# Turning the second pair of hidden column blocks two steps earlier in three feed-forward stages of a hybrid decoder trunk

## The chip, the cores and the metric

The kernel runs on one core of a Trainium2 chip. TensorE (PE in the profile) multiplies matrices, VectorE (DVE) and ScalarE (ACT) do elementwise work, GpSimd (POOL) does a little of it and issues some DMAs, SyncE (SP) issues the weight loads. Each engine works through its own instructions in order and waits for the others through semaphores. The metric is the device time of one execution in microseconds (us). Beside plain timed executions there is one execution recorded by the hardware profiler; its trace is what the views below are taken from.

## The reference

Two layers over 256 tokens of width 1024, everything in float32. Each layer is: a SwiGLU feed-forward (FFN), a token mixer (sparse attention in layer 0, a Mamba-2 scan in layer 1), and a second FFN; after each of the three, a LayerNorm of the scaled residual plus the result. The FFN, which this case is about, is

```python
def swiglu_ffn(x, w_in, w_out):
    gate, up = jnp.split(x @ w_in, 2, axis=-1)
    return (jax.nn.silu(gate) * up) @ w_out
```

with 2816 hidden columns, that is 22 column blocks of 128. There are four FFNs; the mixers lie between the first and second and between the third and fourth.

## The kernel before

**Weights.** A product in float32 is made as three faster passes (`mm3`, L540 to L543): every operand is split into a high part H and a low part L, and H·H, H·L and L·H are added up in one PSUM bank. A weight unit is a 128x1024 tile: SP loads it (`raw`), ACT rounds it to its high part `wh` (L338), DVE subtracts to get the low part `wl` (L363). At most ten units are made ahead of their use. `W.pump`, called once in every step, first emits the low parts of units whose high parts are out, then makes new high parts, then emits sums of raw weight tiles where a block of products needs them (DVE, L305, or an accumulating DMA that POOL issues, L278).

**An FFN.** The 22 column blocks go in this order. First `WIDE = 2` pairs of blocks are made with the tokens on the output rows (`wide`); w = 0 is blocks 0 and 1, w = 1 is blocks 2 and 3. In the FFNs other than the first, four groups of four column blocks follow, each made with seven products in place of eight (a Strassen-type scheme; `seven`). The products of a group are called A11, Q1, S2, Q4, S3, A12 and A22; in the first group of an FFN they run in this order, 12 matmuls each. The last two column blocks are made singly (`one`). In between and behind, `out_pieces` multiplies finished hidden blocks with rows of `w_out` into four accumulator banks `acc00`, `acc01`, `acc10`, `acc11` (two token halves by two column halves), 12 matmuls for each piece, three for each bank. The first group has only two such pieces in it: piece 0 between A12 and A22, piece 1 behind A22.

**Turning.** Hidden values of the wide pairs have tokens on the rows, while `out_pieces` needs columns on the rows. So `tr(w)` (L772) transposes the four 128x128 blocks on PE into one PSUM bank, ACT copies the bank to the high part `hH` (L780), and DVE subtracts to get the low part `hL` (L781), reading the bank as well. For the two wide pairs that bank has the name `pht` and takes the place of an accumulator: w = 0 uses `acc10`, w = 1 uses `acc11`. The accumulators are first written in piece 0, whose last three matmuls go to `acc11`; the tile allocator lets them start only when the bank's earlier reader, the `hL` subtraction, is done.

**What sets the order.** The order is written out by hand through a queue of steps. `later(f, d)` puts work into the d-th step from now, `step()` runs the work of the step that is due and then pumps weights, and there is one step behind each product and each out piece. When the second half of a wide pair is multiplied (`mul`, L789), `tr(w)` is put into the queue; `tr` emits transposes and the ACT copy at once and its DVE subtraction goes to the next step. With a delay of five, counted from the end of the wide products: step one is behind Q1 (it holds `tr(0)`, counted from its own, earlier product), two behind S2, three behind Q4, four behind S3, five behind A12. Step six is behind piece 0. At these places stand also `c12` (L931, emitted in step three), `c22` (L936, step four) and `c11` (L941, step five), subtractions and additions on DVE that put the products together, and the SiLU calls (L787) on ACT.

Of the kernel before, what the change touches and what calls it, by code (L numbers as in the profile page):

```python
# [65 lines left out]
WIDE = 2  # L66
# [353 lines left out]
def trunk_kernel(ctx: ExitStack, tc: tile.TileContext, widths, forms, x, ln_g, ln_b, wts, kvg, convp,  # L420
# [12 lines left out]
    def nm(s):  # L433
        cnt[0] += 1
        return f"{s}_{cnt[0]}"
# [7 lines left out]
    def f1(s):  # L443
        return wk.tile([128, 256], F32, name=nm(s), tag="f1", bufs=6)
# [23 lines left out]
    def ptr():  # L468
        return psum.tile([128, 512], F32, name=nm("ptr"), tag="ptr", bufs=2)
# [276 lines left out]
    def ffn(xT, u0, ln_i, first=False, last=False, ff=False, seven_at=SEVEN):  # L746
# [9 lines left out]
        def later(f, d=1):  # L756

            while len(queue) < d:
                queue.append([])
            queue[d - 1].append(f)  # L760
# [11 lines left out]
        def tr(w):  # L772

            pt = psum.tile([128, 512], F32, name=nm("pht"), tag=f"acc1{w}", bufs=1) if w < WIDE else ptr()
            for t in range(2):
                h = ready.pop((t, w))
                for i in range(2):
                    nc.tensor.transpose(pt[:, i * 256 + t * 128:i * 256 + (t + 1) * 128], h[:, i * 128:(i + 1) * 128],
                                        ident)
            nc.scalar.copy(hH[w], pt)  # L780
            return lambda: nc.vector.tensor_sub(hL[w], pt, hH[w].bitcast(F32))  # L781

        def glu(t, w, c, sil=None):


            g, h = (c[:, :256], c[:, 256:]) if sil is None else (sil, f1("h"))
            nc.scalar.activation(g, c[:, :256], AF.Silu)  # L787

            def mul():  # L789
                nc.vector.tensor_mul(h, c[:, 256:], g)  # L790
                W.owe(800)
                ready[t, w] = h
                if (1 - t, w) in ready:
                    later(lambda: later(tr(w)), 5 if w < WIDE and not first else 2)

            later(mul)

# [971 lines left out]
```

## Time and profile before

| what | value |
|---|---|
| timed executions | 1034.69, 1034.94 and 1036.64 us, median 1034.94 us |
| profiled execution | 1036.55 us |
| its span, first to last instruction | 1034.4 us |
| what lies around the span | 2.15 us |
| PE, DVE, ACT busy (share of the span) | 98%, 88%, 63% |
| mean granted TensorE clock | 0.992 |
| second, third and fourth FFN, from the trace | about 289 to 456, 470 to 636 and 845 to 1028 us |

In a row of the timeline the columns are start, duration, engine, line, operation, output<-inputs, shape, count of merged instructions, and in brackets the idle time of the engine just before with what ended it. PE rows give matmuls, whose modelled durations overlap; the distance from start to start is what counts. In a table of windows each engine has its busy time and, in brackets, its number of instructions; PEclk is the granted TensorE clock, 1.00 being full speed. In the list of waits the columns are total, number of times and longest wait, in us.

### The profile page before, as it was taken

What the parts mean: (1) busy time and instruction counts of PE and PEld (TensorE: products, weight loads), DVE (VectorE), ACT (ScalarE), POOL (GpSimd) and SP (SyncE); (2) the same over time, 40 slices, a digit from 0 to 9 for tenths busy, and PEclk for the clock granted to TensorE, in tenths of its full rate; (3) what the DMA queues carried; (4) which work ended last, traced back from release to release, by engine and by line L of the source; (5) the groups of instructions that cost most, each with busy time, mean ns of one, the idle gap of its engine ahead of it and who ended that gap; (6) DMA issues with size and microseconds to landing.
All of it is one profiled execution on the core that took longest, in us unless ns stands there. A gap on an engine that the chain in (4) does not pass through costs nothing.

```text
span 1034.4 us, 14640 instructions
## 1 busy us (share of the span) xinstructions
PE 1013.6 (98%) x5319; PEld 855.2 (83%) x5319; DVE 911.2 (88%) x1282; ACT 650.5 (63%) x945; POOL 105.4 (10%) x164
## 2 busy tenths in 40 slices
PE   8999999999999999999999999999999999999996
PEld 7888888898787888888788888999889888788885
DVE  6789997788799899979989997789999879989986
ACT  6666675476657666754766675486766546677660
POOL 2011000100001110000111000140111111010001
PEclk9999999999999999999999999999999999999998
DMA  9769998252638889791988988355555645889751
GB/s 334 281 148 286 270 336 294 85 181 75 210 103 243 215 276 276 262 332 66 249 210 282 272 270 286 126 171 193 174 176 178 221 171 121 266 285 261 239 192 42
DMA packets 62505, 223.85 MB, mean 216 GB/s; under 512 B 7040, under 2 KB 7104, under 8 KB 62432
## 3 DMA queue, kind: packets, MB, share of 16 engines
q1 hardware_dynamic: 51264, 183.43, 49.3%
q0 software_dynamic: 10880, 38.96, 18.7%
q8 instruction: 42, 0.69, 0.3%
q10 hardware_dynamic: 288, 0.52, 0.1%
q14 instruction: 31, 0.25, 0.1%
HBM read 193.48 MB, written 1.08 MB: 188 GB/s over the span
## 4 chain that ended last, share of the span: by engine, by line
PE 81%; DVE 10%; ACT 4%; issue 3%; DMA 1%; POOL 0%; SPq 0%; POOLq 0%; DVEq 0%; ACTq 0%
PE pmm L543 10%; PE pmm L541 10%; PE pmm L542 10%; PE acc L541 9%; PE acc L543 9%; PE acc L542 9%; DVE wl L363 4%; ACT wh L338 2%; PE pmm L690 2%; PE ptr L690 2%; PE pxs L541 1%; PE pxs L543 1%; PE pxs L542 1%; PE ptr L542 1%; PE ptr L543 1%
## 5 line engine op out<-in xcount | busy, mean ns | idle before, releaser
L363 DVE TENSOR_TENSOR wl<-raw,wh 128x1024 fp32r<-128x1024 f32 (+2 forms) x422 | 495.2, 1213 | 13.6 <-ACT wh L338 13.3
L338 ACT CAST wh<-raw 128x1024 fp32r<-128x1024 f32 (+2 forms) x424 | 423.1, 1044 | 108.7 <-DVE raw L305 68.9
L541 PE MATMUL acc<-wh,hH 128*128 128x512 f32 (+1 forms) x352 | 139.0, 395 | 7.2 <-DVE hL L781 7.2
L543 PE MATMUL acc<-wh,hL 128*128 128x512 f32 (+1 forms) x352 | 137.3, 390 | 0.0
L542 PE MATMUL acc<-wl,hH 128*128 128x512 f32 (+1 forms) x352 | 137.1, 389 | 0.0
L541 PE MATMUL pmm<-wh,xT 128*128 128x512 f32 (+2 forms) x312 | 123.8, 397 | 0.0
L542 PE MATMUL pmm<-wl,xT 128*128 128x512 f32 (+2 forms) x312 | 120.8, 387 | 0.7 <-DVE wl L363 0.7
L543 PE MATMUL pmm<-wh,xT 128*128 128x512 f32 (+2 forms) x312 | 121.1, 388 | 0.2 <-DVE xT L538 0.2
L278 POOL DMA_DIRECT2D raw<-raw x54 | 47.0, 870 | 408.3 <-DVE raw L305 216.7
L541 PE MATMUL pmm<-wh,xf 128*128 128x512 f32 x216 | 84.4, 391 | 0.1
L543 PE MATMUL pmm<-wh,xf 128*128 128x512 f32 x216 | 84.1, 389 | 0.0
L542 PE MATMUL pmm<-wl,xf 128*128 128x512 f32 x216 | 84.0, 389 | 0.0
L541 PEld LDWEIGHTS acc<-wh,hH 128*128 128x128 f32 x352 | 66.3, 188 | 21.1 <-DVE hL L781 8.5
L305 DVE TENSOR_TENSOR raw<-raw,raw 128x1024 f32<-128x1024 f32 x66 | 79.3, 1220 | 0.4
L543 PEld LDWEIGHTS acc<-wh,hL 128*128 128x128 f32 x352 | 66.4, 189 | 14.0
L542 PEld LDWEIGHTS acc<-wl,hH 128*128 128x128 f32 x352 | 66.5, 189 | 12.5
L543 PEld LDWEIGHTS pmm<-wh,xT 128*128 128x128 f32 x312 | 59.3, 190 | 13.5 <-DVE xT L538 1.6
L542 PEld LDWEIGHTS pmm<-wl,xT 128*128 128x128 f32 x312 | 59.8, 192 | 12.3 <-DVE wl L363 1.4
L541 PEld LDWEIGHTS pmm<-wh,xT 128*128 128x128 f32 x312 | 59.8, 192 | 10.9
L541 PEld LDWEIGHTS pmm<-wh,xf 128*128 128x128 f32 x216 | 40.5, 188 | 8.6 <-ACT c L948 0.3
L543 PEld LDWEIGHTS pmm<-wh,xf 128*128 128x128 f32 x216 | 40.5, 188 | 8.5
L542 PEld LDWEIGHTS pmm<-wl,xf 128*128 128x128 f32 x216 | 40.5, 188 | 8.4
(322 smaller groups left out, 1848.4 us busy)
## 6 DMA issues: line engine op xcount, KB each, us to landing
raw<-in_wts_dram SPq DMA_DIRECT2D x339, 512.0 KB, 5.3
raw<-raw POOLq DMA_DIRECT2D x54, 512.0 KB, 6.1
M<-scr POOLq DMA_DIRECT2D x8, 512.0 KB, 5.2
lng<-in_ln_g_dram POOLq DMA_DIRECT2D x6, 512.0 KB, 5.1
lnb<-in_ln_b_dram POOLq DMA_DIRECT2D x6, 512.0 KB, 5.3
raw<-in_wts_dram SPq DMA_DIRECT2D x4, 408.0 KB, 5.3
out_dram<-x SPq DMA_DIRECT2D x4, 256.0 KB, 2.1
raw<-in_wts_dram SPq DMA_DIRECT2D x2, 492.0 KB, 5.2
```

Source lines behind the costliest of these rows:

```text
L278: self.nc.gpsimd.dma_start(self.raw[r], self.raw[other], accum_op=ALU.add)
L305: self.nc.vector.tensor_add(self.raw[r], self.raw[r], self.raw[other])
L338: nc.scalar.copy(h[:, c:c + n], raw[:, c:c + n])
L363: self.nc.vector.tensor_sub(lo[:, s], raw[:, s], h[:, s].bitcast(F32))
L541: nc.tensor.matmul(ps, lh, rh, start=first, stop=False, skip_group_check=on)
L542: nc.tensor.matmul(ps, lh, rl, start=False, stop=False, skip_group_check=on)
L543: nc.tensor.matmul(ps, ll, rh, start=False, stop=last, skip_group_check=on)
L690: nc.tensor.matmul(ps, H[:, k * 128:(k + 1) * 128], xT.HL[:, k, :], start=k == 0, stop=False)
```

## The change

One expression, in `mul` inside `glu`. The delay of `tr(w)` becomes 5 for w = 0 (as before) and 3 for w = 1. In the first FFN (`first`) and for all other pairs it stays 2.

```diff
                 W.owe(800)
                 ready[t, w] = h
                 if (1 - t, w) in ready:
-                    later(lambda: later(tr(w)), 5 if w < WIDE and not first else 2)
+                    later(lambda: later(tr(w)), 5 - 2 * w if w < WIDE and not first else 2)
```

So in the second, third and fourth FFN the four transposes and the ACT copy of `tr(1)` are emitted in step three (behind Q4) in place of step five (behind A12), and its DVE subtraction in step four (behind S3) in place of step six (behind piece 0). Within step three `tr(1)` stands ahead of `c12`, and its subtraction stands first in step four. No instruction is added or removed; loads, sums and the number of weight units made in each step stay as they are.

## The prediction

> **What bounds the kernel now.** I read the page first, for the engine that carries the time.
>
> ```profile
> span 1034.4 us, 14640 instructions
> PE 1013.6 (98%) x5319; PEld 855.2 (83%) x5319; DVE 911.2 (88%) x1282; ACT 650.5 (63%) x945; POOL 105.4 (10%) x164
> L541 PE MATMUL acc<-wh,hH 128*128 128x512 f32 (+1 forms) x352 | 139.0, 395 | 7.2 <-DVE hL L781 7.2
> ```
>
> PE is busy 98% of the span, so only time in which PE stands still or runs slowly can be won. The third row names such time: the first pass of the out pieces waited 7.2 us for the `hL` subtraction. The list of waits says how often.
>
> ```profile
> PE acc L541 <- DVE hL L781: 7.2, 3, 2.4
> ```
>
> Three waits of 2.4 us, and three FFNs have a delay of five. The PE timeline of the second FFN shows the place.
>
> ```profile
> 324.97 0.39 PE L543 MATMUL ptr<-wh,xf 128*128 128x512 f32 x1
> ...
> 330.41 0.39 PE L543 MATMUL ptr<-wh,xT 128*128 128x512 f32 x1
> 330.64 0.60 PE L778 MATMUL pht<-ident,h 128*128 128x128 f32 x4
> 330.99 0.48 PE L541 MATMUL acc<-wh,hH 128*128 128x512 f32 x1
> ...
> 332.93 0.40 PE L543 MATMUL acc<-wh,hL 128*128 128x512 f32 x1
> 335.71 0.79 PE L541 MATMUL acc<-wh,hH 128*128 128x512 f32 x1 [2.39 <-DVE hL L781]
> ...
> 338.86 0.39 PE L542 MATMUL pmm<-wl,xT 128*128 128x512 f32 x1
> ```
>
> 324.97 is the last matmul of Q4, 330.41 the last of A12, 24 matmuls later: (330.41 - 324.97) / 24 = 0.227 us from start to start. Then come the transposes of `tr(1)`, nine matmuls of piece 0, and a stop before the tenth, the first into `acc11`, the bank that `tr(1)` still holds. DVE and ACT in the same time:
>
> ```profile
> 317.68 0.42 DVE L790 TENSOR_TENSOR h<-pmm,sil 128x256 f32<-128x256 f32 x1
> ...
> 326.44 2.35 DVE L363 TENSOR_TENSOR wl<-raw,wh 128x1024 fp32r<-128x1024 f32 x2
> 328.89 0.69 DVE L937 TENSOR_TENSOR c<-c 128x512 f32<-128x512 f32 x1
> 329.50 2.35 DVE L363 TENSOR_TENSOR wl<-raw,wh 128x1024 fp32r<-128x1024 f32 x2
> ...
> 334.98 0.68 DVE L781 TENSOR_TENSOR hL<-pht,hH 128x512 fp32r<-128x512 f32 x1
> ```
>
> ```profile
> 324.45 3.92 ACT L338 CAST wh<-raw 128x1024 fp32r<-128x1024 f32 x4
> 328.25 0.61 ACT L967 COPY c<-pmm 128x512 f32<-128x512 f32 x1
> ...
> 331.42 0.58 ACT L780 CAST hH<-pht 128x512 fp32r<-128x512 f32 x1
> ```
>
> `hH` is out at 332.00, but the subtraction stands behind other work in DVE's queue and ends at 334.98 + 0.68 = 335.66; PE goes on at 335.71. So the release is the subtraction and nothing later.
>
> **The second price of the wait** is in the clock. Windows cut at the clock's changes, one for each site:
>
> ```profile
> 335.44:338.85 3.41, 3.13 (x7) 2.48 (x8) 3.41 (x5) 0.00 (x0) 0.00 (x0) 0.50 1.02 408
> 516.34:519.76 3.42, 3.42 (x8) 2.69 (x9) 3.42 (x4) 0.00 (x0) 0.00 (x0) 0.50 1.03 412
> 891.81:895.22 3.41, 3.41 (x10) 2.64 (x9) 3.41 (x4) 0.10 (x1) 0.00 (x0) 0.50 1.02 410
> ```
>
> After each wait the granted clock is 0.50 for 3.41 us. [...] The other two sites look the same:
>
> ```profile
> 513.50 0.39 PE L543 MATMUL acc<-wh,hL 128*128 128x512 f32 x1
> 516.26 0.75 PE L541 MATMUL acc<-wh,hH 128*128 128x512 f32 x1 [2.38 <-DVE hL L781]
> ...
> 519.79 0.39 PE L543 MATMUL pmm<-wh,xT 128*128 128x512 f32 x1
> ...
> 888.55 0.39 PE L543 MATMUL acc<-wh,hL 128*128 128x512 f32 x1
> 891.35 0.50 PE L541 MATMUL acc<-wh,hH 128*128 128x512 f32 x1 [2.42 <-DVE hL L781]
> ...
> 895.33 0.39 PE L542 MATMUL pmm<-wl,xT 128*128 128x512 f32 x1
> ```
>
> **The change part by part.** *The wait.* Start to start less one regular step: 335.71 - 332.93 - 0.23 = 2.55; 516.26 - 513.50 - 0.23 = 2.53; 891.35 - 888.55 - 0.23 = 2.57. Sum 7.65 us.
>
> *The slow stretch.* From the resuming matmul to the first back at a regular distance there are 7, 8 and 10 steps: 3.15 - 7 x 0.227 = 1.56; 3.53 - 8 x 0.227 = 1.71; 3.98 - 10 x 0.227 = 1.71. Sum 4.98 us. It goes only if the idle time that brings it goes.
>
> *Transposes moved to behind Q4.* They cost PE 330.99 - 330.64 = 0.35 us in either place. Their input is ready: the second half's multiplication ends at 318.10, PE gets there at 325.19. Nothing is paid, and no DMA is moved past.
>
> *ACT copy moved.* It now stands between the second and third of the four casts from 324.45. ACT is there at 324.45 + 2 x 0.95 = 326.35; the transposes end at about 325.8. So ACT doesn't wait, by about 0.5 us, and PE's lateness would have to grow by that before ACT and all weights behind it stood waiting. The copy takes 331.90 - 331.42, about 0.48 us of ACT, and the casts and the u3 copy (L967) behind it come that much later, until its old place.
>
> *Subtraction moved.* It takes 0.60 us of DVE (0.68 with the overlap) and goes ahead of `c22` (L937). The low part before it ends at 328.79, its `hH` at about 326.9, so it ends at about 329.4. PE wants `acc11` at 332.93 + 0.23 = 333.16: 3.7 us to spare, in place of 2.5 too late. But `c22` waits for the u3 copy, too, and goes from 328.89 to about 329.35, and the two low parts from 329.50 to about 329.96. The first of them is the weight of piece 0: out at 330.72 before, needed at piece 0's second matmul, 330.99 + about 0.32 = 331.31. Of 0.59 us to spare 0.46 are used. Bounds: nothing, or all of 0.48 + 0.60 in series, which is 0.49 us of wait at each site. I take 0.1, as the work is in two queues that overlap.
>
> *What is late next.* PE now reaches A22 and the next group about 4.1 us earlier, while DVE was at work through the whole wait.
>
> ```profile
> 341.30 0.42 DVE L790 TENSOR_TENSOR h<-pmm,sil 128x256 f32<-128x256 f32 x1 [0.43 <-ACT sil L787]
> 341.64 3.49 DVE L363 TENSOR_TENSOR wl<-raw,wh 128x1024 fp32r<-128x1024 f32 x3
> ...
> 350.62 0.69 DVE L781 TENSOR_TENSOR hL<-ptr,hH 128x512 fp32r<-128x512 f32 x1 [1.49 <-ACT hH L780]
> 351.57 5.77 DVE L363 TENSOR_TENSOR wl<-raw,wh 128x1024 fp32r<-128x1024 f32 x5 [0.26 <-ACT wh L338]
> ```
>
> ```profile
> 349.51 0.59 ACT L949 COPY c<-pmm 128x512 f32<-128x512 f32 x1 [2.08 <-PE pmm L543]
> ```
>
> ```profile
> 346.81 0.39 PE L542 MATMUL pmm<-wl,xf 128*128 128x512 f32 x1
> ...
> 354.11 0.39 PE L542 MATMUL pmm<-wl,xf 128*128 128x512 f32 x1
> ```
>
> The low part from 341.64 (Q1 of the second group) ends at 342.86 and is used at 346.81: 3.95 to spare, less 4.1, would be just late. DVE comes to it 0.43 us earlier, since the wait ahead of it, for a SiLU that needs PE's A22, goes; about 0.3 is left. The low part from 351.57 ends at 352.79 and is used at 354.11: 1.32 to spare. DVE gets there earlier by 0.43, by its gap of 1.49, which was a wait for ACT while ACT waited for PE (2.08), by the 0.26, and by 0.60 - 0.46 = 0.14 that the moved subtraction leaves over: 2.3 of the 4.1 us. 1.32 + 2.3 - 4.1 is about -0.5. After that the DVE row that waits for PE's next product puts both in step again. I take 0.3 here, between none and 0.5: 0.4 us in all for each site, 1.2 us; bounds 0 and, if DVE doesn't move at all, 4.1 - 1.32 = 2.8 for each site.
>
> *Sum*, against the profiled execution's own 1036.55 us (span 1034.40 and 2.15 around it): 1036.55 - 7.65 - 4.98 + 1.2 = 1025.1 us. The median of the timed runs, 1034.94, is 1.6 lower. The timed runs lie 1.95 apart, close to one slow stretch (1.56 to 1.71): if the faster two had a stretch less, the new time is 1025.1 whatever the old one was; if a profiled execution is merely longer, it is 1034.94 - 11.43 = 1023.5. The highest timed run equals the profiled one, so I lean to the first and say **1024.7 us**.
>
> **The rivals.**
>
> *A, a partial hold by DVE.* The wait moves to the row at 354.11, where 1.32 us were to spare, and DVE, 88% busy, doesn't get earlier. Of the 4.1 us only 1.32 are left at that row, and PE waits 2.8 us, more than the 2.39 that halved the clock, so that a new slow stretch of 1.66 (the mean of the three) follows. Net -0.34 for each site, 1036.55 + 1.0 = 1037.6: no change. Against it stand the gaps of 1.49 and 2.08, both waits that end with PE. If the clock isn't halved at the new place, 1036.55 - 3 x 1.32 = 1032.6.
>
> *B, the clock drop has another cause and stays.* 1036.55 - 7.65 + 1.2 = 1030.1. Against it: the clock is halved during the work three times, each right behind one of these waits.
>
> *C, slower.* The bank isn't what holds PE, but DVE's queue up to that point; then the moved copy and subtraction are put ahead of weights that PE needs, and pay in full: 0.48 + 0.60 for each site, 3 x 1.08 = 3.2, that is 1039.8 us. It decides if the tenth matmul of piece 0 still starts at the end of whatever row DVE now has where the subtraction stood at 334.98. Against it: PE resumes 0.05 us behind L781.
>
> *D, the change doesn't do what it says:* another reader of `acc11` holds the bank, 1036.5. The sums of the input's transposed halves read it last, before the wide products' end, so little speaks for it.
>
> **How the numbers follow.** Forecast 0.78 (its own range 1022.3 to 1026.6: the lower base with no loss, 1023.5 - 1.2, and the upper with a loss of 0.9 in place of 0.4 for each site, 1025.1 + 1.5), A without halving 0.04 and with it 0.05, B 0.07, C 0.04, D 0.02. About 0.2% (2 us) is what a measurement of this kernel can tell from no change. Faster: 0.78 + 0.04 + 0.07 = 0.89; the same: 0.05 + 0.02 = 0.07; slower 0.04. The range takes in B: 1021.5 to 1030.5.
>
> **What the profile of the changed kernel would show.** Right: no wait of L541 for L781 in the list; the transposes into `pht` behind Q4, their ACT copy right after two casts, and the subtraction ahead of L937; piece 0 as twelve matmuls 0.23 us apart; mean clock near 1.00 with no window of 0.50 between the start and the end; PE waits for L363 of up to 0.5 us in the second group. Wrong: an idle time of over 1 us before an L542 row in the second group (A), full gaps gone but windows of 0.50 left (B), a wait at piece 0's tenth matmul (C, D), or ACT waiting for `pht`.

## The result, and the profile after

| | before | after |
|---|---|---|
| timed executions, median (lowest to highest) | 1034.94 us (1034.59 to 1036.64) | 1025.76 us (1024.76 to 1026.83) |
| ratio | | 0.9909, 95% interval 0.9894 to 0.9923 |
| profiled execution | 1036.55 us | 1026.70 us |
| its span | 1034.4 us | 1024.5 us |
| mean granted TensorE clock | 0.992 | 0.998 |

The kernel became 0.9% faster. 1024.7 us was forecast, 1.1 us below the median. From the page after:

```profile
span 1024.5 us, 14640 instructions
PE 1010.8 (99%) x5319; PEld 853.3 (83%) x5319; DVE 910.3 (89%) x1282; ACT 649.1 (63%) x945; POOL 105.2 (10%) x164
...
L541 PE MATMUL acc<-wh,hH 128*128 128x512 f32 (+1 forms) x352 | 138.0, 392 | 0.0
...
L542 PE MATMUL pmm<-wl,xf 128*128 128x512 f32 x216 | 84.7, 392 | 0.9 <-DVE wl L363 0.8
```

The same 14640 instructions; the 7.2 us of idle time ahead of the first pass of the out pieces is 0.0. The list of waits no longer has L541 waiting for L781. What grew in its place are waits for low parts (total, times, longest; before there was one, of 0.7 us, at the start of the execution):

```profile
PE pmm L542 <- DVE wl L363: 0.8, 3, 0.4
```

The PE timeline of the second FFN, around the same place as in the prediction:

```profile
325.48 0.39 PE L543 MATMUL ptr<-wh,xf 128*128 128x512 f32 x1
325.71 0.60 PE L778 MATMUL pht<-ident,h 128*128 128x128 f32 x4
326.06 0.48 PE L541 MATMUL pmm<-wh,xf 128*128 128x512 f32 x1
...
333.46 0.39 PE L543 MATMUL acc<-wh,hL 128*128 128x512 f32 x1
333.69 0.39 PE L541 MATMUL acc<-wh,hH 128*128 128x512 f32 x1
...
350.82 0.51 PE L542 MATMUL pmm<-wl,xf 128*128 128x512 f32 x1
```

The transposes stand behind Q4 and cost 0.35 us there, as they did behind A12. The ninth and the tenth matmul of piece 0 are 0.23 us apart, where there were 2.78. The last row, in the second group, is 0.53 us behind its predecessor at 350.29 in place of 0.23. ACT and DVE:

```profile
324.93 2.02 ACT L338 CAST wh<-raw 128x1024 fp32r<-128x1024 f32 x2
326.84 0.60 ACT L780 CAST hH<-pht 128x512 fp32r<-128x512 f32 x1
```

```profile
329.18 0.68 DVE L781 TENSOR_TENSOR hL<-pht,hH 128x512 fp32r<-128x512 f32 x1
329.85 0.69 DVE L937 TENSOR_TENSOR c<-c 128x512 f32<-128x512 f32 x1
...
349.55 5.75 DVE L363 TENSOR_TENSOR wl<-raw,wh 128x1024 fp32r<-128x1024 f32 x5
```

The copy follows two casts without a gap. The subtraction is ahead of L937 and ends at 329.86, 3.83 us before PE wants the bank at 333.69. The row at 349.55 is the one that was at 351.57: DVE comes there 2.02 us earlier, and its first low part ends where PE goes on, at about 350.8.

The clock, in windows of the trace after, from where it comes up to shortly before the end (PEclk is the third number from the right):

```profile
11.10:333.00 321.90, 321.17 (x1760) 269.76 (x1759) 279.58 (x466) 209.12 (x342) 23.78 (x32) 1.00 0.66 215
333.00:340.00 7.00, 7.00 (x33) 5.77 (x32) 7.00 (x9) 1.79 (x4) 0.00 (x0) 1.00 1.03 414
340.00:1021.00 681.00, 674.07 (x3500) 570.42 (x3498) 619.56 (x803) 433.43 (x594) 75.98 (x113) 1.00 0.70 218
```

No slow stretch is left between the start and the end.

**Where the time went.** Both kernels issue the same products in the same order (only the transposes moved), so the same matmul can be set against itself. Four rows of before, beside those that the prediction shows:

```profile
356.15 0.39 PE L542 MATMUL pmm<-wl,xf 128*128 128x512 f32 x1
...
537.11 0.39 PE L543 MATMUL pmm<-wh,xf 128*128 128x512 f32 x1
...
912.19 0.39 PE L543 MATMUL pmm<-wh,xf 128*128 128x512 f32 x1
...
943.07 0.39 PE L543 MATMUL pmm<-wh,xf 128*128 128x512 f32 x1
```

And the same matmuls after, with those that answer to 338.86, 519.79 and 895.33 in the prediction:

```profile
335.27 0.39 PE L542 MATMUL pmm<-wl,xT 128*128 128x512 f32 x1
...
353.02 0.40 PE L542 MATMUL pmm<-wl,xf 128*128 128x512 f32 x1
...
512.46 0.39 PE L543 MATMUL pmm<-wh,xT 128*128 128x512 f32 x1
...
530.22 0.39 PE L543 MATMUL pmm<-wh,xf 128*128 128x512 f32 x1
...
884.29 0.39 PE L542 MATMUL pmm<-wl,xT 128*128 128x512 f32 x1
...
901.57 0.39 PE L543 MATMUL pmm<-wh,xf 128*128 128x512 f32 x1
...
930.84 0.50 PE L542 MATMUL pmm<-wl,xf 128*128 128x512 f32 x1 [0.45 <-DVE wl L363]
...
933.24 0.39 PE L543 MATMUL pmm<-wh,xf 128*128 128x512 f32 x1
```

| stretch | after less before at its end | change in it |
|---|---|---|
| start to Q4 of the second FFN | 325.48 - 324.97 = +0.51 | +0.51 |
| second FFN, wait and slow stretch | 335.27 - 338.86 = -3.59 | -4.10 |
| its second group | 353.02 - 356.15 = -3.13 | +0.46 |
| third FFN, wait and slow stretch | 512.46 - 519.79 = -7.33 | -4.20 |
| its second group | 530.22 - 537.11 = -6.89 | +0.44 |
| fourth FFN, wait and slow stretch | 884.29 - 895.33 = -11.04 | -4.15 |
| its second group | 901.57 - 912.19 = -10.62 | +0.42 |
| its third group | 933.24 - 943.07 = -9.83 | +0.79 |

Won: 4.10 + 4.20 + 4.15 = 12.45 us. Given back: 0.46 + 0.44 + 0.42 = 1.32 in the second groups and 0.79 in one third group (0.61 there in the second profiled execution of the change, below). The 0.51 at the start is older than the first site: there the clock came up to full at 7.76 us before and at 11.02 us after (matmuls of 512 columns are 0.23 us apart from 7.77 on before, and still 0.43 us apart up to 10.79 after).

The 0.79 goes by way of a DMA. In the fourth FFN, POOL issues a sum of raw weights and ACT casts its result; before:

```profile
912.25 0.89 POOL L278 DMA_DIRECT2D raw<-raw  x1 [1.31 <-DVE wl L363]
...
922.01 2.00 ACT L338 CAST wh<-raw 128x1024 fp32r<-128x1024 f32 x2 [2.01 <-DMA raw<-raw]
```

and after:

```profile
902.73 0.89 POOL L278 DMA_DIRECT2D raw<-raw  x1 [1.32 <-DVE wl L363]
...
912.59 2.00 ACT L338 CAST wh<-raw 128x1024 fp32r<-128x1024 f32 x2 [3.21 <-DMA raw<-raw]
```

PE is 10.62 us earlier there. The issue, which waits for a low part of DVE, is 912.25 - 902.73 = 9.52 earlier, and so ACT waits 1.2 us longer, and low parts behind that come late: at 930.84 PE waits 0.45 us for one.

### The profile page after: what moved, and what is told of

It reads as the page before. It is cut to its first block, busy times and chain, and to the rows that moved or that the text cites. A ratio compares the mean times of both kernels' runs of the same rounds, so it can differ in the third digit from the quotient of the medians.

```text
span 1024.5 us, 14640 instructions
## 1 busy us (share of the span) xinstructions
PE 1010.8 (99%) x5319; PEld 853.3 (83%) x5319; DVE 910.3 (89%) x1282; ACT 649.1 (63%) x945; POOL 105.2 (10%) x164
## 4 chain that ended last, share of the span: by engine, by line
PE 80%; DVE 14%; issue 3%; DMA 1%; ACT 1%; POOL 0%; POOLq 0%; DVEq 0%; ACTq 0%
PE pmm L543 10%; PE pmm L542 10%; PE pmm L541 10%; PE acc L541 8%; PE acc L543 8%; PE acc L542 8%; DVE wl L363 6%; DVE raw L305 3%; PE pmm L690 2%; PE ptr L690 2%; PE ptr L542 2%; PE ptr L543 2%; PE ptr L541 2%; PE pxs L541 2%; PE pxs L543 1%
## 5 line engine op out<-in xcount | busy, mean ns | idle before, releaser
L363 DVE TENSOR_TENSOR wl<-raw,wh 128x1024 fp32r<-128x1024 f32 (+2 forms) x422 | 494.7, 1212 | 13.8 <-ACT wh L338 13.7
L541 PE MATMUL acc<-wh,hH 128*128 128x512 f32 (+1 forms) x352 | 138.0, 392 | 0.0
L542 PE MATMUL acc<-wl,hH 128*128 128x512 f32 (+1 forms) x352 | 136.7, 388 | 0.0
L541 PE MATMUL pmm<-wh,xT 128*128 128x512 f32 (+2 forms) x312 | 122.9, 394 | 0.0
L542 PE MATMUL pmm<-wl,xT 128*128 128x512 f32 (+2 forms) x312 | 120.4, 386 | 0.0
L542 PE MATMUL pmm<-wl,xf 128*128 128x512 f32 x216 | 84.7, 392 | 0.9 <-DVE wl L363 0.8
L541 PE MATMUL pmm<-wh,xf 128*128 128x512 f32 x216 | 84.8, 393 | 0.1
L542 PEld LDWEIGHTS acc<-wl,hH 128*128 128x128 f32 x352 | 66.3, 188 | 13.2 <-DVE wl L363 0.4
L541 PEld LDWEIGHTS acc<-wh,hH 128*128 128x128 f32 x352 | 66.2, 188 | 12.7
L542 PEld LDWEIGHTS pmm<-wl,xT 128*128 128x128 f32 x312 | 59.2, 190 | 11.0 <-DVE wl L363 0.3
L541 PEld LDWEIGHTS pmm<-wh,xT 128*128 128x128 f32 x312 | 59.2, 190 | 10.4
L542 PEld LDWEIGHTS pmm<-wl,xf 128*128 128x128 f32 x216 | 40.6, 188 | 10.9 <-DVE wl L363 2.8
L541 PEld LDWEIGHTS pmm<-wh,xf 128*128 128x128 f32 x216 | 40.6, 188 | 8.6 <-ACT c L948 0.3
```

Of the source, the lines that this page charges most:

```text
L363: self.nc.vector.tensor_sub(lo[:, s], raw[:, s], h[:, s].bitcast(F32))
L541: nc.tensor.matmul(ps, lh, rh, start=first, stop=False, skip_group_check=on)
L542: nc.tensor.matmul(ps, lh, rl, start=False, stop=False, skip_group_check=on)
```

## The experiments

The theory: the bank `acc11`, held until the `hL` subtraction ends, stops PE at the tenth matmul of piece 0; the idle time brings the slow stretch; what is given back is DVE's lateness. The rivals are those of the prediction, above all B (another cause of the clock drop) and C (DVE's queue, not the bank). Each group of runs was timed beside the kernel before: 1035.57 us for the first four experiments, 1035.43 for the next four, 1035.58 for the last.

**The change once more.**

> The changed kernel once more, beside the kernels of this group. Theory (the bank of the second turned pair held the first out piece; the halved clock came of that wait): about 9 to 10 us faster than before, ratio 0.991, no wait of the first out piece for the subtraction, no stretch of half clock in the middle. If part of the gain came of the start of the execution, where the clock comes up at a time that differs from one execution to the next, the ratio moves by up to 0.001 between groups of runs.

Measured: 1026.26 us, ratio 0.9906 (0.9892 to 0.9919), span 1023.7 us. The waits for low parts at L542 sum to 1.0 us (0.8 above).

**A delay of four.**

```diff
-                    later(lambda: later(tr(w)), 5 if w < WIDE and not first else 2)
+                    later(lambda: later(tr(w)), 5 - w if w < WIDE and not first else 2)
```

> The second pair turned four steps behind its product. Its subtraction then stands in step five, first behind A12, and still ahead of the first out piece. Theory (only the place of the subtraction relative to the first out piece matters): no wait, gain as with three, 9 to 10 us, and the low part of the first out piece's weight comes some 0.5 us earlier than with three, so at most 0.1 us for each site better than with three. Rival (each step nearer to the product counts): half the gain, about 5 us. Rival (the subtraction is too late for the bank, as PE reaches it at about 333.2 and DVE ends it at about 332.4 with 0.8 us to spare): a wait again, of less than 0.5 us.

Measured: 1025.86 us, ratio 0.9905 (0.989 to 0.992), the same as the change. One step is enough. Against the change, by the starts of the same matmuls, PE wins 0.79 us in the fourth FFN's third group, so that loss is not a necessary one.

**Another bank at the old place.** The delay stays five; in the three FFNs `tr(1)` gets a bank of the rotating `ptr` in place of `acc11`.

```diff
-            pt = psum.tile([128, 512], F32, name=nm("pht"), tag=f"acc1{w}", bufs=1) if w < WIDE else ptr()
+            pt = psum.tile([128, 512], F32, name=nm("pht"), tag=f"acc1{w}", bufs=1) if w < (WIDE if first else 1) else ptr()
```

> Delay five as before, but the second pair is turned in one of the two banks that later pairs use, so that the accumulator bank is free; transposes, ACT copy and subtraction stand where they stood before. Theory (the bank is what held PE): the three waits of 2.4 us and the three stretches of half clock go, gain as with the change, 9 to 10 us, ratio 0.991. Rival C (DVE's queue up to that point held PE): the waits stay and the time is that of before, ratio 1.000.

Measured: 1026.4 us, ratio 0.9907 (0.9894 to 0.9921). Its timeline, DVE and then PE:

```profile
335.04 0.68 DVE L781 TENSOR_TENSOR hL<-ptr,hH 128x512 fp32r<-128x512 f32 x1
```

```profile
333.02 0.39 PE L543 MATMUL acc<-wh,hL 128*128 128x512 f32 x1
333.25 0.39 PE L541 MATMUL acc<-wh,hH 128*128 128x512 f32 x1
```

The subtraction is as late as before (335.04, before 334.98), at its old place in DVE's queue, and the tenth matmul starts 1.8 us ahead of it without a wait. So the bank held PE, and DVE's queue did not: C falls, and the time won doesn't come from the new order of ACT and DVE.

**The order of the change for PE and ACT, the subtraction as late as before.** Transposes and copy in step three, the subtraction in step six.

```diff
-                    later(lambda: later(tr(w)), 5 if w < WIDE and not first else 2)
+                    if w == 1 and not first:
+                        later(lambda: later(tr(w), 3), 3)
+                    else:
+                        later(lambda: later(tr(w)), 5 if w < WIDE and not first else 2)
```

> Transposes and ACT copy of the second pair in step three as in the change, but the subtraction in step six, where it was before. Theory (the subtraction releases the bank): the waits stay at 2.3 to 2.5 us with the half clock behind each, time as before, ratio 0.999 to 1.001. Rival (it was the transposes or the ACT copy that came too late): most of the gain stays, ratio 0.991 to 0.993.

Measured: 1038.2 us, ratio 1.0022 (1.0013 to 1.0031). The list of waits, and windows at the first two sites:

```profile
PE acc L541 <- DVE hL L781: 8.8, 3, 2.9
```

```profile
333.50:334.68 1.18, 0.00 (x0) 0.00 (x0) 1.18 (x2) 0.89 (x2) 0.00 (x0) 1.00 1.04 424
334.68:336.41 1.73, 0.00 (x1) 0.03 (x1) 1.73 (x3) 0.00 (x0) 0.00 (x0) 1.00 1.03 419
336.41:340.00 3.59, 3.59 (x16) 2.95 (x17) 3.59 (x5) 0.00 (x0) 0.00 (x0) 1.00 1.02 406
515.59:519.00 3.41, 2.82 (x7) 2.27 (x8) 3.41 (x5) 0.00 (x0) 0.00 (x0) 0.50 1.02 408
```

The whole gain is gone: it hangs on the subtraction alone. The expected waits came, 0.5 us longer than before's, and the ratio lies a little above the 0.999 to 1.001 that was expected. But at the first site PE was idle for 2.91 us (1.18 + 1.73), longer than at any site of before, and the clock stayed at 1.00 behind it. The other two sites, with 2.9 us as well, were halved. More idle time and less slow time: the length of the wait alone doesn't decide.

The slow stretches lie on a grid. In before they are 3.41 to 3.42 us long and begin at 335.44, 516.34 and 891.81, and their distances are 53 and 110 steps of that length: 180.90 / 53 = 3.413 and 375.47 / 110 = 3.413. In this run the two begin at 515.59 and 891.06, 375.47 us apart as well. Fifty-three steps (180.91 us) back from 515.59, the grid of this run has a line at 334.68, in the middle of the first wait: 1.18 us of it lie in one step, or window, and 1.73 in the next. Before's first wait, from 333.33 to 335.71, had 2.11 us within the window that ends at 335.44, and the clock was halved from there. So 2.11 us idle within one window had a half clock behind them, and 1.73 had none. The end of before narrows this further. Its last matmul is

```profile
1026.19 0.28 PE L543 MATMUL pmm<-wh,hL 128*128 128x256 f32 x1
```

and the clock falls at 1028.34, again on the grid (136.53 us, 40.0 windows, behind 891.81): there 1.87 us idle, from 1026.47 on, had it behind them.

**The wait left in place, but filled.** At piece 0 of the three FFNs ten more matmuls, into a free bank that nobody reads, stand between the ninth and the tenth.

```diff
-                    out_k(acc, t, *lhs(jj, t), u, jj == 0, False)
+                    if t and jj == 0 and not first:
+                        H, L = W.get(u)
+                        lh, ll = lhs(jj, t)
+                        mm3(acc[t][0], lh, ll, H[:, :512], L[:, :512], True, False)
+                        fill = ptr()
+                        for _ in range(10):
+                            nc.tensor.matmul(fill, lh, H[:, :512], start=True, stop=True)
+                        mm3(acc[t][1], lh, ll, H[:, 512:], L[:, 512:], True, False)
+                    else:
+                        out_k(acc, t, *lhs(jj, t), u, jj == 0, False)
```

> The kernel before, with the wait left in place and filled: between the ninth and the tenth matmul of the first out piece PE makes ten matmuls more (512 columns, some 2.27 us) into a free bank; nobody reads them, and the output is unchanged. Theory (the halved clock comes of the idle time): idle 0.1 to 0.4 us in place of 2.4, no stretch of half clock, and the kernel is faster by the slow stretches alone, 1.6 to 1.7 us for each that an execution of the kernel before has: 3 to 5 us, ratio 0.995 to 0.998. Rival B (the clock drop has another cause): stretches of half clock stay, ratio 1.000.

Measured: 1031.71 us, ratio 0.9963 (0.9949 to 0.9976), span 1029.4. Its PE timeline:

```profile
332.55 0.39 PE L543 MATMUL acc<-wh,hL 128*128 128x512 f32 x1
332.78 2.43 PE L870 MATMUL ptr<-wh,hH 128*128 128x512 f32 x10
335.33 0.50 PE L541 MATMUL acc<-wh,hH 128*128 128x512 f32 x1
```

The tenth matmul is as late as before relative to the ninth (335.33 - 332.55 = 2.78, before 335.71 - 332.93 = 2.78), and no window of 0.50 is left between start and end. Windows around the three sites:

```profile
333.00:338.00 5.00, 4.88 (x22) 3.71 (x21) 5.00 (x7) 1.14 (x2) 0.00 (x0) 1.00 1.03 418
...
510.00:525.00 15.00, 14.85 (x67) 11.96 (x67) 15.00 (x18) 8.37 (x13) 1.71 (x2) 1.00 0.96 311
885.00:900.00 15.00, 14.88 (x68) 11.98 (x67) 15.00 (x18) 6.86 (x10) 1.74 (x2) 1.00 0.88 275
```

The two prices come apart. By the spans, this run is 1034.4 - 1029.4 = 5.0 us shorter than before, of which 332.93 - 332.55 = 0.38 are older than the first site (the ninth matmul of piece 0); so about 4.6 us are left for the clock (the prediction has 4.98). The wait is the rest: the change is 1029.4 - 1024.5 = 4.9 us shorter still, though it was 333.46 - 332.55 = 0.91 behind at that matmul, so from there on it wins about 5.8 us, net of what it gives back. By the medians this run is 1035.43 - 1031.71 = 3.7 us faster than before; the section on the prediction comes back to the spread of before. Rival B falls, since work without use in the idle time removed the slow stretches.

**A delay of two.**

```diff
-                    later(lambda: later(tr(w)), 5 if w < WIDE and not first else 2)
+                    later(lambda: later(tr(w)), 5 - 3 * w if w < WIDE and not first else 2)
```

> The second pair turned two steps behind its product, behind S2. Theory: the bank is free in time here too, so most of the gain stays, but the ACT copy and the subtraction now stand ahead of weights that PE waits for already (0.05 to 0.7 us to spare behind S2): up to 0.5 us lost for each site against three steps, ratio 0.991 to 0.9925. Rival (earlier is better): 0.990 or less.

Measured: 1026.13 us, ratio 0.9906 (0.9892 to 0.992), as with three and four. The loss of up to 0.5 us for each site that was expected did not come: in its profiled execution the small shifts cancel out.

**The subtraction one step later than before.** Step seven in place of step six.

```diff
-                    later(lambda: later(tr(w)), 5 if w < WIDE and not first else 2)
+                    later(lambda: later(tr(w), 2 if w == 1 and not first else 1), 5 if w < WIDE and not first else 2)
```

> The kernel before with the subtraction one step later still, in step seven: DVE has two low parts and two sums more to do ahead of it, so that it ends about 4.8 us later. Theory (the end of the subtraction sets when PE goes on): each of the three waits grows from 2.4 to about 7.2 us, time 14 to 17 us above before, ratio 1.013 to 1.017; a wait of 7.2 us holds a whole idle window of 3.41 us wherever it falls, so all three sites have a half clock behind them. Rival C (a place in DVE's queue other than the subtraction): the waits don't grow, ratio near 1.000.

Measured: 1053.43 us, ratio 1.0169 (1.0155 to 1.0182). The list of waits and the windows of the three slow stretches, with the idle time of PE ahead of the first:

```profile
PE acc L541 <- DVE hL L781: 21.8, 3, 7.3
```

```profile
333.22:337.39 4.17, 0.00 (x1) 0.00 (x0) 4.17 (x5) 1.21 (x2) 0.00 (x0) 1.00 1.03 418
337.39:344.22 6.83, 3.72 (x9) 2.95 (x10) 3.39 (x5) 1.04 (x1) 1.71 (x2) 0.50 0.95 260
...
521.71:531.95 10.24, 5.72 (x14) 4.47 (x15) 4.80 (x6) 1.04 (x1) 1.71 (x2) 0.50 0.95 265
904.01:910.83 6.82, 3.62 (x9) 2.84 (x10) 3.48 (x5) 1.05 (x1) 1.73 (x2) 0.50 0.97 271
```

The ratio is at the upper end of the forecast; in time, 1053.43 - 1035.43 = 18.0 us, a little above the 14 to 17. The wait moves with the subtraction, by (21.8 - 7.2) / 3 = 4.9 us in the mean. All three sites have a half clock behind them: at the first, PE was idle through the whole window that ends at 337.39, where the clock falls. The stretches are two, three and two windows of 3.41 us, for waits of 7.3 us in the mean and at most: again the place on the grid. In the second stretch PE was busy for 5.72 us, so it was back at about 531.95 - 5.72 = 526.23, some 1.1 us into the window that begins at 525.12 by the grid, and the following window, 528.54 to 531.95, was slow all the same. So within this slow stretch a window with some 1.1 us idle had another slow one behind it.

**The change without two DVE sums** at the beginning of the second group in these FFNs. The run leaves out these sums of raw weights, so the product that uses them is made with an incomplete weight.

```diff
-                self.nc.vector.tensor_add(self.raw[r], self.raw[r], self.raw[other])
+                if u not in (137, 138, 227, 228, 375, 376):
+                    self.nc.vector.tensor_add(self.raw[r], self.raw[r], self.raw[other])
```

> The changed kernel without the two sums of raw weight tiles on DVE (1.15 us each) at the start of the second group of the second, third and fourth FFN; Q1 of that group is then made with the tile that lacks the second summand, so this part of the result is not computed. Theory (in the second group PE waits because DVE, 2.3 us behind, is late with one low part): the wait of 0.3 us there goes and with it about 0.5 us for each site: 1 to 2 us less than the changed kernel, ratio 0.989 to 0.9905. Rival (the wait there comes of a load or of an accumulating DMA): it stays, 0.9905 to 0.991.

Measured: 1023.86 us, ratio 0.9885 (0.9872 to 0.9899). At the place where the change has its step of 0.53 us (the line numbers are one higher here):

```profile
350.20 0.39 PE L542 MATMUL pmm<-wh,xf 128*128 128x512 f32 x1
350.42 0.39 PE L543 MATMUL pmm<-wl,xf 128*128 128x512 f32 x1
```

0.22 us, a regular step. Set against the change by the same matmuls, this run wins 0.47, 0.48 and 0.46 in the second groups and 0.79 in the fourth FFN's third group. That is as much as the change gave back, the 0.79 too, so it was DVE's lateness in both.

**DVE relieved.** The change, with 36 multiplications of the products' halves (L790) on GpSimd in place of DVE.

```diff
-                nc.vector.tensor_mul(h, c[:, 256:], g)
+                (nc.vector if sil is not None or first else nc.gpsimd).tensor_mul(h, c[:, 256:], g)
```

> The changed kernel with the multiplication of the product-made halves (128x256, SBUF to SBUF, 0.42 us on DVE, three in each group) given to GpSimd in the second, third and fourth FFN. Theory (DVE is late by 0.3 us with one low part in the second group): DVE is relieved of 2 x 0.33 us ahead of that low part, PE's wait there goes, 1.5 to 2.3 us less than the changed kernel, ratio 0.989 to 0.9895. Rival (GpSimd's multiplication is slow, stands behind its DMA issues, or slows DVE's own instructions beside it): no gain or a loss, ratio 0.991 or more.

Measured: 1035.2 us, ratio 0.9993 (0.9984 to 1.0002). The whole gain is lost. Groups of lines of this run and its list of waits:

```profile
L363 DVE TENSOR_TENSOR wl<-raw,wh 128x1024 fp32r<-128x1024 f32 (+2 forms) x422 | 513.2, 1256 | 13.1 <-ACT wh L338 12.8
...
L790 POOL TENSOR_TENSOR c<-c 128x256 f32<-128x256 f32 x36 | 53.1, 1475 | 154.4 <-ACT c L787 154.4
```

```profile
PE pmm L542 <- DVE wl L363: 4.7, 10, 1.2
```

After the change, the first of these groups is:

```profile
L363 DVE TENSOR_TENSOR wl<-raw,wh 128x1024 fp32r<-128x1024 f32 (+2 forms) x422 | 494.7, 1212 | 13.8 <-ACT wh L338 13.7
```

DVE gives away 36 multiplications, by 0.417 us each 15.0 us, but its 422 subtractions, which the edit doesn't touch, take 513.2 - 494.7 = 18.5 us more, and a multiplication takes 1.48 us on GpSimd in the mean. PE waits for low parts of products ten times, in place of three. With the six waits at L542 for other tiles (`ptr`, 2.0 us in three, and `acc`, 0.9 us in three) it is 7.6 us in place of 0.8, of the 1033.7 - 1024.5 = 9.2 us that this run is longer. So the rival of the expectation holds; how much of the loss comes of the slower subtractions, how much of the slow multiplications themselves, was not separated.

## Why the prediction was right

*The wait, 7.65 us, and the slow stretch, 4.98 us.* Right in mechanism and size: 12.63 forecast, 12.45 by the starts of the same matmuls. Another bank at the old place shows the cause of the first, the filled wait shows the second and gives it alone about 4.6 us. What the prediction didn't have is the grid: it took idle time of 2.39 us as the cause, but 2.91 us, cut by a line of the grid, cost no slow stretch.

*Transposes and ACT copy at nothing.* Right: 0.35 us in either place, the copy behind two casts without a gap.

*Weight of piece 0, 0.1 us for each site.* Smaller: the second and third matmul of piece 0 start at regular steps in the second FFN and up to 0.05 us late in the fourth. It lies within the 12.45.

*What is late next, 0.3 us for each site.* The place was right (the row at 354.11, now 350.82) and so was the sign of DVE's lag: 2.3 of PE's 4.1 us forecast. Measured are 351.57 - 349.55 = 2.02, to which come the 0.51 us by which this execution was already late, so about 2.5 of PE's 4.10; 1.32 + 2.5 - 4.1 is -0.3. At the row itself the loss is 350.82 - 350.29 - 0.23 = 0.30, as taken, but the matmuls behind it lose some more, so that the group's loss was nearer to the bound of 0.5: 0.46, 0.44 and 0.42, in sum 1.32. All losses together had been put at 1.2.

*What the sum lacked.* The 0.79 us in the fourth FFN's third group: DVE's lag also delays an accumulating DMA, which the prediction didn't follow past the second group. And the 0.51 at the start, where the clock came up later in this one execution. 1025.1 + 0.51 + 0.79 + (1.32 - 1.2) + (12.63 - 12.45) = 1026.7, the profiled execution after. Profiled against profiled, the gain was 1036.55 - 1026.70 = 9.85 us where 11.43 was forecast; that the forecast came within 1.1 us of the median is owed in part to luck, since the median after is 0.9 below the profiled execution.

*The base.* The two readings were a slow stretch less in the faster timed runs, and a profiled execution that is merely longer. The mean clock of the timed executions speaks for the first: of the fifteen of before beside the first experiments, three had 0.992 like the profiled one and took 1036.2 to 1036.6 us, one had 0.993 and took 1037.7, and eleven had 0.994 or 0.995 and took 1034.7 to 1035.9. One stretch lowers the mean clock by 3.41 x 0.5 / 1034 = 0.0017, so 0.994 would answer to about one stretch less than 0.992. But the slow time at the very end enters the mean as well: the two profiled executions of the change have no such stretch, and 0.998 and 0.997. So the mean clock alone does not tell. The time around the span is 2.1 to 2.2 us in either kind. Against the second reading speaks that the profiled execution was the shortest of its group in four of the experiments (the change once more, the delay of four, and both with a later subtraction). That waits fall on the grid differently in each execution would explain it, but only the profiled ones show the clock over time, so it is argued and not shown. The rest of the spread has another source: after the change the timed executions still lie 2.07 us apart, at 0.997 to 0.998. The time at which the clock first comes up (7.8 to 11.0 us in the profiles) can be part of it; the whole is open.

*The rivals.* A: the wait did move to the row named, with 0.3 us there and 0.4 to 0.5 in all, and not 2.8, since DVE became earlier with PE. B and C fell by experiments. D fell with the result: no reader but the subtraction held the bank.

## What to carry to other kernels

The PSUM bank that was lent to a short job here was returned at the place that its last reader had in that reader's queue (335.66 us), and not when the data were ready (332.00). In such a case give the job another bank (1026.4 us here) or put the last reader a step ahead, and one step was as good as three (1025.86 and 1025.76 us). Three waits of about 2.5 us in a stream of matmuls cost some 60% as much again in the clock here (about 4.6 us for 7.65 of waits), and matmuls into a free bank, with the wait left in place, saved that part. Whoever moves PE forward should follow the next busy engine for two groups of work, its releases of DMAs included.

## What was not expected of the hardware

- Whether a wait had a half clock behind it went with how it lay on a grid of 3.413 us: 2.11 us within one window had, and at the end of the execution 1.87; 2.91 us cut into 1.18 and 1.73 had not. Slow stretches were one, two or three windows long (3.41, 6.83, 10.24 us).
- The kernel with longer waits thus had fewer slow stretches: two in the profiled execution of the run with 2.9 us waits, three in that of before with 2.4.
- Multiplications of 128x256 on GpSimd took 1.48 us in the mean (0.417 on DVE), and in that run DVE's subtractions took 1256 ns in place of 1212, in the mean of all 422.
